# The last four heads' output product by blocks of tokens, its weights in free slots, and the residual's affine step behind the column split

## The chip, the cores and the metric

The kernel runs on one core of a Trainium2 chip. Its time is the device time of one execution in microseconds, the median over runs. A core has TensorE (PE, matrix products, with weight loads as PEld), VectorE (DVE), ScalarE (ACT), GpSimd (POOL) and SyncE (SP, which here issues most DMAs). Each engine works through its own queue in order and waits on semaphores for the others.

## The reference

The program is two small transformer-like blocks of two layers each over 256 latent and 256 context tokens of width 1024. The change touches the end of the first layer (windowed attention with 16 heads) and the beginning of the second (a state-space layer, S5):

```python
o, oc = attention_mixer(p, pc, sink, row, col, True)          # 16 heads of 128
x  = layer_norm(alpha * x  + gate   * ((o  * silu(z))  @ w_out[0]), ln_g[0], ln_b[0])
xc = layer_norm(alpha * xc + gate_c * ((oc * silu(zc)) @ w_out[0]), ln_g[0], ln_b[0])
# layer 1
h  = x  * (1 + scale)   + shift
hc = xc * (1 + scale_c) + shift_c
pz = h @ s5_w_in ; pzc = hc @ s5_w_in                          # then the S5 scan, its gate, w_out[1]
x  = layer_norm(alpha * x + gate * (...), ln_g[1], ln_b[1])
```

## The kernel before

The tokens are four blocks of 128 (0 and 1 latent, 2 and 3 context). All products run in single precision split in two: a value is a high half (rounded, made by ACT, `copy_a`) and a low half (value minus high half, made by a subtraction on DVE or POOL, `sub`), and `mm3` issues three matmuls, high x high, high x low, low x high. A weight unit (`wunit`) is a DMA into one of 6 slots of pool ST, then a high and a low half in one of 3 slots of pool WL. `lo_pat` names, unit by unit, the engine of the low half ("V" for DVE, "P" for POOL).

`l0_attention` runs over the 16 heads: `scores(h + 1)`, `values(h)`, some steps of side generators that prepare the S5 layer, after every fourth head the output product `out_proj(g)` of a finished group of four, and `heads(h + 3)`, the projections of a later head. The product is accumulated in `acc[b]`, one 128x1024 tile for each block. `residual()` multiplies the first three groups' sum by the gate and adds alpha times x. The last group, `out_proj(3)`, comes behind the loop: for each column half `nh`, four blocks `b`; each (nh, b) is 12 matmuls, a product with the gate, a sum into `acc` and `stat` (bn_stats) on DVE. Then `layer_norm` for blocks 0 and 1, and for 2 and 3: thirteen tiny DVE instructions for mean and 1/sigma of two blocks, then one scaling each, on DVE and on ACT. Gain and bias of this norm are not applied here; they are folded into the next layer's columns.

`block1_l1` begins layer 1. `fm_part` transposes the normed blocks (PE), two blocks at a time, latent first, into eight column tiles hT; for each of 8 x 2 parts ACT makes the high half, DVE the scaled value (L384) and, here always DVE, the low half (L385). Beside it POOL does the affine step for the residual, x * ln_g + ln_b, in place on the two latent blocks (L1198 and L1199), and SP stores it to `xrd`, which is read at the end of layer 1. Then `s5_mix` runs its stages in the order of a string: u0 (the first input product, 4 weight units, 96 matmuls), a step of z0, t0, z0, x0, u1, and so on.

Pool E has 8 slots of 128x1024; in layer 0 they hold the eight column tiles of the attention's input, which the projections read. Pool H has 16 such slots. Pools SB and E are closed behind layer 0, and layer 1's pool S5 takes their memory.

The order on each engine is not written out by hand. The program is in the order of the source, and the framework's planner lays out each engine's queue by simulated time (L2030): what is ready and stands earlier in the program goes first. Slots of pools are given out in the same way.

Of the kernel before, what the change touches and what calls it, by code (L numbers as in the profile page):

```python
# [5 lines left out]
F32 = mybir.dt.float32  # L6
F32R = mybir.dt.float32r
# [3 lines left out]
ALU = mybir.AluOpType  # L11
# [94 lines left out]
def bc(ap, *dims):  # L106

    return bass.AP(tensor=ap.tensor, offset=ap.offset, ap=[list(ap.ap[0])] + [list(d) for d in dims])


class Builder:
# [37 lines left out]
        self.nc.scalar.activation(o, i, AF.Copy)  # L149

    def sub(self, o, a, b, eng=None):
        (eng or self.nc.vector).tensor_tensor(o, a, b, op=ALU.subtract)  # L152

    def add(self, o, a, b, eng=None):
        (eng or self.nc.vector).tensor_tensor(o, a, b, op=ALU.add)  # L155

    def mul(self, o, a, b, eng=None):
        (eng or self.nc.vector).tensor_tensor(o, a, b, op=ALU.mult)  # L158

    def ts(self, o, a, s1, op0, s2=None, op1=None, eng=None):  # L160
        e = eng or self.nc.vector
# [198 lines left out]
    def fm_part(self, out, c0, toks, A, B, chunked=False):  # L360


        nc = self.nc
        w = 128 * len(toks)
        m = 512 // w
        for kp in range(8 // m):
            ps = self.pms()
            for k in range(m):
                for b, t in enumerate(toks):
                    kt = m * kp + k  # L370
                    nc.tensor.transpose(ps[:, k * w + b * 128:k * w + (b + 1) * 128], t[:, kt * 128:(kt + 1) * 128],
                                        self.ident)
            h = self.qslot()
            for k in range(m):
                kt = m * kp + k
                sl = slice(k * w, (k + 1) * w)
                src, tmp = ps[:, sl], h[:, sl]
                if chunked:
                    hi, lo = (bc(out[kt][:, r, c0:c0 + 1], (64, 8), (1, 32)) for r in range(2))
                    src, tmp = (bc(t, (1, 8), (8, 32)) for t in (src, tmp))  # L380
                else:
                    hi, lo = (out[kt][:, r, c0:c0 + w] for r in range(2))
                nc.scalar.activation(hi, src, AF.Identity, bias=B(kt), scale=A(kt))
                self.ts(h[:, sl], ps[:, sl], A(kt), ALU.mult, B(kt), ALU.add)  # L384
                self.sub(lo, tmp, hi, nc.gpsimd if k % 2 and not chunked else None)  # L385
            yield

    def layer_norm(self, toks, stats=None, gain=None, bias=None):
# [26 lines left out]
    def l0_attention(self, hT, vps, W, sink, negsink, Wo, gates, ada):  # L415
        nc = self.nc
# [29 lines left out]
        acc, Ks, pend, yz = [], {}, {}, {}  # L446
        sc = 128 ** -0.5

        def heads(h):

            g = h // 4
            if h % 4 == 0:
                Ks[g] = rope(proj(2048 + g * 128))
            q = rope(proj(h * 128))
            zps = proj(3072 + h * 128)
            th = self.qslot()
            nc.scalar.activation(th, zps, AF.Tanh, scale=0.5)
            self.stt(th, th, 1.0, zps, ALU.add, ALU.mult)
            pend[h] = [q, th]
# [46 lines left out]
        def values(h):  # L506
            P, th = pend.pop(h)
            g = h // 4
            PT = []
            for u in range(3):  # L510
                pp = self.pms()
                for k in range(2):
                    for b in range(2):
                        src = P[b][:, (2 * u + k) * 128:(2 * u + k + 1) * 128] if u < 2 else \
                            P[2][:, b * 256 + k * 128:b * 256 + (k + 1) * 128]
                        nc.tensor.transpose(pp[:, k * 256 + b * 128:k * 256 + (b + 1) * 128], src, self.ident)
                if u != 1:
                    pt = self.hslot()
                o = pt[:, 512 * (u % 2):512 * (u % 2 + 1)]
                self.copy_a(o, pp)  # L520
                PT += [o[:, :256], o[:, 256:]]
            yp = self.pms()
            vs = slice(g * 128, (g + 1) * 128)
            for kb in range(4):
                nc.tensor.matmul(yp[:, :256], V[kb][:, vs], PT[kb], start=kb == 0, stop=kb == 3)
            for kb in range(2):
                nc.tensor.matmul(yp[:, 256:], V[2 + kb][:, vs], PT[4 + kb], start=kb == 0, stop=kb == 1)
            self.stt(th, th, 0.5, yp, ALU.mult, ALU.mult)
            y = self.hslot(F32R)[:, :].rearrange("p (a b) -> p a b", a=2)
            self.split(y, th, lo_eng=self.off)  # L530
            yz[h] = y

        def out_proj(g):
            y = [yz.pop(4 * g + k) for k in range(4)]
            if g == 0:
                acc.extend(self.hslot() for _ in range(4))
            gt = gates_
            for nh in range(2):
                ws = [self.w_as(Wo, g * 4 + 2 * u, (nh * 512, 512)) for u in range(2)]
                for b in range(4):  # L540
                    ps = self.pacc()
                    for k in range(4):
                        self.mm3(ps, (y[k][:, 0, b * 128:(b + 1) * 128], y[k][:, 1, b * 128:(b + 1) * 128]),
                                 ws[k // 2][k % 2], k == 0, k == 3)
                    a = acc[b][:, nh * 512:(nh + 1) * 512]
                    if g == 0:
                        self.copy_a(a, ps)
                    elif g < 3:
                        self.add(a, a, ps)
                    else:  # L550
                        t = self.qslot()
                        self.mul(t, ps, gt[b // 2][:, nh * 512:(nh + 1) * 512])
                        self.add(a, a, t)
                        stat(b, nh)

        def residual():

            gates_.extend(gates())
            for b in range(4):
                xt = self.hslot()  # L560
                self.dma(xt, (self.I["x"][0] if b < 2 else self.I["ctx"][0])[(b % 2) * 128:(b % 2 + 1) * 128, :])
                nc.scalar.activation(xt, xt, AF.Copy, scale=ALPHA)
                self.mul(acc[b], acc[b], gates_[b // 2])
                self.add(acc[b], acc[b], xt)

        def stat(b, nh):
            if nh == 0:
                stats[b] = self.T.tile([128, 2, 6], F32, tag="bn", name="bn")
            nc.vector.bn_stats(stats[b][:, nh, :], acc[b][:, nh * 512:(nh + 1) * 512])

        gates_, stats = [], {}
# [7 lines left out]
        for h in range(16):  # L579
            if h < 15:  # L580
                scores(h + 1)
            values(h)
            for k, gen in SIDE[h]:
                for _ in range(k):
                    next(side[gen], None)
            if h % 4 == 1 and h > 3:
                out_proj(h // 4 - 1)
                if h == 13:
                    residual()
            if h + LEAD < 16:  # L590
                heads(h + LEAD)
        self.lo_pat = "P"
        out_proj(3)
        for b in (0, 2):
            self.layer_norm(acc[b:b + 2], [stats[b], stats[b + 1]])
        return acc

    def block1_l0(self):
# [580 lines left out]
    def block1_l1(self):  # L1179
        nc, I = self.nc, self.I  # L1180
        v, at = self.v1, self.v1at
        mod = self.mod1
        A = self.C.tile([128, 2, 2, 8], F32, name="A1")
        for q in range(2):
            g, b = v[:, at["ln_g"]:at["ln_g"] + 8], v[:, at["ln_b"]:at["ln_b"] + 8]
            self.stt(A[:, q, 0, :], mod[:, 8:16, q], 1.0, g, ALU.add, ALU.mult)
            self.stt(A[:, q, 1, :], mod[:, 8:16, q], 1.0, b, ALU.add, ALU.mult)
            self.add(A[:, q, 1, :], A[:, q, 1, :], mod[:, 0:8, q])
        x = self.x1
        hT = [self.hslot(F32R)[:, :].rearrange("p (a b) -> p a b", a=2) for _ in range(8)]  # L1190
        for q in range(2):
            for _ in self.fm_part(hT, 32 * (1 - q), x[2 * q:2 * q + 2], lambda k: A[:, q, 0, k:k + 1], lambda k: A[:, q, 1, k:k + 1], True):
                pass

        xrd = self.DR.tile([256, 1024], F32, name="xrd")
        gb, bb = self.row_bc(I["ln_g"][0]), self.row_bc(I["ln_b"][0])
        for b in range(2):
            self.mul(x[b], x[b], gb, nc.gpsimd)  # L1198
            self.add(x[b], x[b], bb, nc.gpsimd)  # L1199
            self.dma(xrd[b * 128:(b + 1) * 128, :], x[b])  # L1200
        self.xrd = xrd
        return self.s5_mix(hT, I["s5_w_in"][0])
# [831 lines left out]
```

## Time and profile before

| | us |
|---|---|
| median of 3 runs (2323.80 to 2330.18) | 2326.35 |
| the profiled execution | 2329.09 |
| its span | 2327.2 |
| PE busy | 2030.9 |
| DVE busy | 1429.4 |
| ACT busy | 875.5 |
| POOL busy | 749.3 |

The span is what the profiler saw from the first to the last instruction; the execution's own time holds 1.9 us around it. Times within the span count from its start. The seam between the two layers lies between 600 and 745 us.

### The profile page before, as it was taken

What the parts mean: (1) busy time and instruction counts of PE and PEld (TensorE: products, weight loads), DVE (VectorE), ACT (ScalarE), POOL (GpSimd) and SP (SyncE); (2) the same over time, 40 slices, a digit from 0 to 9 for tenths busy, and PEclk for the clock granted to TensorE, in tenths of its full rate; (3) what the DMA queues carried; (4) which work ended last, traced back from release to release, by engine and by line L of the source; (5) the groups of instructions that cost most, each with busy time, mean ns of one, the idle gap of its engine ahead of it and who ended that gap; (6) DMA issues with size and microseconds to landing.
All of it is one profiled execution on the core that took longest, in us unless ns stands there. A gap on an engine that the chain in (4) does not pass through costs nothing. (4 is left out here: it accounts for less than half of the span.)

```text
span 2327.2 us, 34638 instructions
## 1 busy us (share of the span) xinstructions
PE 2030.9 (87%) x13236; PEld 1597.8 (69%) x13236; DVE 1429.4 (61%) x2945; ACT 875.5 (38%) x1650; POOL 749.3 (32%) x501
## 2 busy tenths in 40 slices
PE   5697788999987878659888899999999999988998
PEld 3575565677766676547786565778888877657997
DVE  5788887766695867564547735553333466455556
ACT  2234233334434453534434243343222244334443
POOL 1687877800013201323333210122111513112334
PEclk9897877999998987879999979999999999889999
DMA  7656535544554576989465606433333226354663
GB/s 265 181 181 204 182 110 162 154 164 140 187 165 117 184 182 168 233 193 289 145 231 161 189 15 234 138 91 91 105 95 93 89 75 184 133 175 134 191 190 118
DMA packets 362775, 368.56 MB, mean 158 GB/s; under 512 B 27512, under 2 KB 291420, under 8 KB 362608
## 3 DMA queue, kind: packets, MB, share of 16 engines
q1 hardware_dynamic: 356048, 355.32, 50.9%
q0 software_dynamic: 2208, 6.29, 0.9%
q10 hardware_dynamic: 4352, 4.72, 0.6%
q8 instruction: 105, 1.72, 0.3%
q14 instruction: 62, 0.51, 0.1%
HBM read 319.62 MB, written 46.65 MB: 157 GB/s over the span
## 5 line engine op out<-in xcount | busy, mean ns | idle before, releaser
L149 ACT ACTIVATE wl<-st 128x1024 fp32r<-128x1024 f32 (+1 forms) x332 | 344.4, 1043 | 491.7 <-PE pa L202 165.7
L152 POOL TENSOR_TENSOR wl<-st,wl 128x1024 fp32r<-128x1024 f32 (+1 forms) x98 | 237.3, 2422 | 873.9 <-ACT wl L149 846.8
L152 DVE TENSOR_TENSOR wl<-st,wl 128x1024 fp32r<-128x1024 f32 (+1 forms) x234 | 321.3, 1376 | 269.2 <-ACT wl L149 268.4
L200 PE MATMUL pa<-h,wl 128*128 128x512 f32 (+1 forms) x1152 | 403.5, 353 | 10.5 <-DVE q L158 6.4
L202 PE MATMUL pa<-h,wl 128*128 128x512 f32 (+1 forms) x1152 | 401.6, 350 | 8.0 <-DVE wl L152 7.6
L201 PE MATMUL pa<-h,wl 128*128 128x512 f32 (+1 forms) x1152 | 402.9, 351 | 0.0
L200 PEld LDWEIGHTS pa<-h,wl 128*128 128x128 f32 x1152 | 220.3, 192 | 46.4 <-issue 7.9
L202 PEld LDWEIGHTS pa<-h,wl 128*128 128x128 f32 x1152 | 220.5, 192 | 38.7 <-DVE wl L152 8.7
L201 PEld LDWEIGHTS pa<-h,wl 128*128 128x128 f32 x1152 | 220.8, 192 | 27.8 <-issue 0.2
L201 PE MATMUL pa<-wl,h 128*128 128x512 f32 (+1 forms) x560 | 224.5, 404 | 16.8 <-DVE wl L152 15.3
L200 PE MATMUL pa<-wl,h 128*128 128x512 f32 (+1 forms) x560 | 218.9, 407 | 18.6 <-ACT wl L149 7.4
L202 PE MATMUL pa<-wl,h 128*128 128x512 f32 (+1 forms) x560 | 215.3, 400 | 9.8 <-DVE h L152 5.7
L152 POOL TENSOR_TENSOR h<-q,h 128x256 fp32r<-128x256 f32 (+2 forms) x82 | 95.3, 1170 | 213.4 <-ACT h L149 137.1
L168 DVE SCALAR_TENSOR_TENSOR q<-q,pa 128x512 f32<-128x512 f32 (+1 forms) x104 | 58.9, 567 | 166.7 <-ACT q L1861 91.7
L149 ACT ACTIVATE h<-pm 128x512 f32<-128x512 f32 (+3 forms) x182 | 93.0, 545 | 170.0 <-PE pm L1529 46.4
L201 PE MATMUL pm<-wl,h 128*128 128x512 f32 (+1 forms) x376 | 146.6, 393 | 2.7 <-DVE wl L152 2.0
L200 PEld LDWEIGHTS pa<-wl,h 128*128 128x128 f32 x560 | 110.2, 199 | 55.0 <-ACT h L149 11.4
L202 PE MATMUL pm<-wl,h 128*128 128x512 f32 (+1 forms) x376 | 143.2, 393 | 0.0
L201 PEld LDWEIGHTS pa<-wl,h 128*128 128x128 f32 x560 | 111.7, 199 | 45.3 <-DVE wl L152 18.1
L299 PE MATMUL pf<-st,cs 128*32 128x512 f32 x576 | 98.2, 688 | 50.8 <-DMA st<-in_w_ada_dram 25.0
L200 PE MATMUL pm<-wl,h 128*128 128x512 f32 (+1 forms) x376 | 139.6, 391 | 1.0 <-ACT wl L149 1.0
L202 PEld LDWEIGHTS pa<-wl,h 128*128 128x128 f32 x560 | 109.8, 198 | 35.7 <-DVE h L152 7.2
(352 smaller groups left out, 3768.4 us busy)
## 6 DMA issues: line engine op xcount, KB each, us to landing
st<-in_w_ada_dram SPq DMA_DIRECT2D x96, 512.0 KB, 5.3
st<-in_ada_w_dram SPq DMA_DIRECT2D x48, 512.0 KB, 5.7
st<-in_w_ffn_gate_dram SPq DMA_DIRECT2D x44, 512.0 KB, 4.2
st<-in_w_ffn_up_dram SPq DMA_DIRECT2D x44, 512.0 KB, 3.9
st<-in_w_ffn_down_dram SPq DMA_DIRECT2D x44, 512.0 KB, 3.7
st<-in_attn_w_in_dram SPq DMA_DIRECT2D x40, 512.0 KB, 4.8
st<-in_w_out_dram SPq DMA_DIRECT2D x40, 512.0 KB, 4.0
wd<-w SPq DMA_DIRECT2D x64, 256.0 KB, 4.3
```

The lines of the kernel that those rows point to most:

```text
L149: self.nc.scalar.activation(o, i, AF.Copy)
L152: (eng or self.nc.vector).tensor_tensor(o, a, b, op=ALU.subtract)
L168: self.nc.vector.scalar_tensor_tensor(o, a, s, b, op0=op0, op1=op1)
L200: mm(o, w[0], x[0], start=start, stop=False)
L201: mm(o, w[0], x[1], start=False, stop=False)
L202: mm(o, w[1], x[0], start=False, stop=stop)
L299: mm = nc.tensor.matmul(ps[32 * q:32 * q + 32, :], self.cs[:, blk, kt, :, :], st[:, (q % 2) * 512:(q % 2 + 1) * 512], start=k0 == 0, stop= ...
```

## The change

1. `out_proj` is now only called for the first three groups. Its last-group branch is gone.
2. `last_weights()` loads and splits the last group's four weight units after head 14's values: DMA into ST, high half on ACT, low half on DVE, both into slots of pool E, not of WL.
3. `last_proj()` runs the last product with the blocks outside and the column halves inside, and norms two blocks as soon as both are complete.
4. POOL's first product of the affine step gets an added dependence on the last low half of the columns (`self.last_fm`), and `sub` and `mul` return their instruction for that.

```diff
-                self.sub(lo, tmp, hi, nc.gpsimd if k % 2 and not chunked else None)
+                self.last_fm = self.sub(lo, tmp, hi, nc.gpsimd if k % 2 and not chunked else None)
...
                     if g == 0:
                         self.copy_a(a, ps)
-                    elif g < 3:
+                    else:
                         self.add(a, a, ps)
-                    else:
-                        t = self.qslot()
-                        self.mul(t, ps, gt[b // 2][:, nh * 512:(nh + 1) * 512])
-                        self.add(a, a, t)
-                        stat(b, nh)
+
+        def last_weights():
+
+            ws = []
+            for nh, u in itertools.product(range(2), range(2)):
+                st = self.ST.tile([128, 1024], F32, tag="st", name="st")
+                src = Wo[(12 + 2 * u) * 128:(14 + 2 * u) * 128, nh * 512:nh * 512 + 512].rearrange("(k p) n -> p k n", p=128)
+                self.dma(st[:, :].rearrange("p (a b) -> p a b", b=512), src)
+                hi, lo = (self.hslot(F32R, True) for _ in range(2))
+                self.copy_a(hi, st)
+                self.sub(lo, st, hi)
+                ws.append([(hi[:, k * 512:k * 512 + 512], lo[:, k * 512:k * 512 + 512]) for k in range(2)])
+            return ws
+
+        def last_proj(ws):
+
+            y = [yz.pop(12 + k) for k in range(4)]
+            for b in range(4):
+                for nh in range(2):
+                    ps = self.pacc()
+                    for k in range(4):
+                        self.mm3(ps, (y[k][:, 0, b * 128:(b + 1) * 128], y[k][:, 1, b * 128:(b + 1) * 128]),
+                                 ws[2 * nh + k // 2][k % 2], k == 0, k == 3)
+                    cs = slice(nh * 512, nh * 512 + 512)
+                    t = self.qslot()
+                    self.mul(t, ps, gates_[b // 2][:, cs])
+                    self.add(acc[b][:, cs], acc[b][:, cs], t)
+                    stat(b, nh)
+                if b % 2:
+                    self.layer_norm(acc[b - 1:b + 1], [stats[b - 1], stats[b]])
...
             values(h)
+            if h == 14:
+                lw = last_weights()
...
         self.lo_pat = "P"
-        out_proj(3)
-        for b in (0, 2):
-            self.layer_norm(acc[b:b + 2], [stats[b], stats[b + 1]])
+        last_proj(lw)
         return acc
...
         for b in range(2):
-            self.mul(x[b], x[b], gb, nc.gpsimd)
+            m = self.mul(x[b], x[b], gb, nc.gpsimd)
+            self.tc.add_manual_dep(m.ins, self.last_fm.ins.name,
+                                   mybir.DependencyInfo(mybir.DependencyClass.Sync, mybir.DependencyReason.DATA),
+                                   reason="after the columns")
             self.add(x[b], x[b], bb, nc.gpsimd)
```

## Rows read from the trace of the kernel before

**Rows 1.** Busy time by stretch: stretch, length, busy us (instructions) of PE, PEld, DVE, ACT, POOL, then PEclk, DMA share, GB/s.

```profile
606.00:618.00 12.00, 12.00 (x111) 8.32 (x105) 3.21 (x8) 4.22 (x10) 0.00 (x0) 1.00 0.71 244
...
640.00:680.00 40.00, 32.26 (x232) 24.13 (x231) 36.60 (x58) 16.76 (x31) 4.76 (x2) 0.87 0.50 171
...
679.30:695.20 15.90, 15.89 (x99) 12.45 (x98) 14.54 (x28) 3.87 (x5) 2.54 (x2) 1.00 0.55 146
...
710.00:728.60 18.60, 13.77 (x48) 10.47 (x47) 18.53 (x24) 6.05 (x11) 10.72 (x5) 0.72 0.40 149
728.60:742.00 13.40, 13.40 (x60) 11.07 (x59) 1.23 (x1) 3.96 (x13) 4.56 (x2) 1.00 0.28 89
...
742.00:2327.20 1585.20, 1411.69 (x9585) 1146.17 (x9583) 862.80 (x2045) 615.63 (x1101) 398.31 (x265) 0.92 0.52 152
```

**Rows 2.** Timeline of PE: start, duration, engine, line, operation, count, idle before with its releaser.

```profile
602.94 0.40 PE L202 MATMUL pa<-h,wl 128*128 128x512 f32 x1
...
653.42 0.80 PE L200 MATMUL pa<-wl,h 128*128 128x512 f32 x1 [3.95 <-DVE h L155]
...
702.76 3.68 PE L371 MATMUL pm<-cst,h 128*128 128x128 f32 x16 [7.58 <-DVE h L165]
...
722.41 1.65 PE L202 MATMUL pa<-wl,h 128*128 128x512 f32 x3 [4.05 <-DVE h L152]
...
741.78 0.39 PE L202 MATMUL pm<-wl,h 128*128 128x512 f32 x1
```

**Rows 3.** Timeline of DVE.

```profile
644.18 3.39 DVE L158 TENSOR_TENSOR h<-h 128x1024 f32<-128x1024 f32 x1
...
649.23 3.39 DVE L158 TENSOR_TENSOR h<-h 128x1024 f32<-128x1024 f32 x1
...
678.62 0.68 DVE L152 TENSOR_TENSOR h<-q,h 128x512 fp32r<-128x512 f32 x1
...
713.26 1.13 DVE L152 TENSOR_TENSOR h<-q,h 128x256 fp32r<-128x256 f32 x2
...
720.18 5.28 DVE L152 TENSOR_TENSOR h<-q,h 128x256 fp32r<-128x256 f32 x3
```

**Rows 4.** Costliest groups on DVE, 679.3 to 728.6 us: busy, mean ns, idle before.

```profile
L152 DVE TENSOR_TENSOR h<-q,h 128x256 fp32r<-128x256 f32 x16 | 16.0, 1031 | 0.0
L165 DVE TENSOR_SCALAR q<-pm,A 128x256 f32<-128x256 f32 x16 | 8.1, 541 | 0.4 <-ACT h L383 0.4
L155 DVE TENSOR_TENSOR h<-h,q 128x512 f32<-128x512 f32 x8 | 5.4, 681 | 0.0
L569 DVE BATCH_NORM_STATS2 bn<-h 128x6 f32<-128x512 f32 x8 | 5.4, 679 | 0.0
L158 DVE TENSOR_TENSOR q<-pa,h 128x512 f32<-128x512 f32 x8 | 5.2, 677 | 1.3 <-PE pa L202 1.2
L152 DVE TENSOR_TENSOR wl<-st,wl 128x1024 fp32r<-128x1024 f32 x2 | 2.4, 1213 | 0.0
```

**Rows 5.** Timeline of POOL.

```profile
644.08 2.41 POOL L152 TENSOR_TENSOR wl<-st,wl 128x1024 fp32r<-128x1024 f32 x1 [12.43 <-ACT wl L149]
649.20 2.35 POOL L152 TENSOR_TENSOR wl<-st,wl 128x1024 fp32r<-128x1024 f32 x1 [2.70 <-ACT wl L149]
...
714.42 4.99 POOL L158 TENSOR_TENSOR h<-h 128x1024 f32<-128x1024 f32 x2 [16.90 <-DVE h L152]
719.37 5.17 POOL L155 TENSOR_TENSOR h<-h 128x1024 f32<-128x1024 f32 x2
728.00 2.77 POOL L152 TENSOR_TENSOR wl<-st,wl 128x1024 fp32r<-128x1024 f32 x1 [3.46 <-ACT wl L149]
```

**Rows 6.** Timeline of SP's DMA issues.

```profile
605.90 2.29 SPq L146 DMA_DIRECT2D st<-in_w_out_dram  x4
...
691.91 11.55 SPq L146 DMA_DIRECT2D m<-kd  x16
...
721.99 2.90 SPq L146 DMA_DIRECT2D xrd<-h  x2
...
733.73 7.00 SPq L146 DMA_DIRECT2D st<-wd  x3
```

More of the change, by code (lines that the diff above doesn't have):

```diff
@@ L151, in sub @@
     def sub(self, o, a, b, eng=None):
-        (eng or self.nc.vector).tensor_tensor(o, a, b, op=ALU.subtract)
+        return (eng or self.nc.vector).tensor_tensor(o, a, b, op=ALU.subtract)
     def add(self, o, a, b, eng=None):
@@ L157, in mul @@
     def mul(self, o, a, b, eng=None):
-        (eng or self.nc.vector).tensor_tensor(o, a, b, op=ALU.mult)
+        return (eng or self.nc.vector).tensor_tensor(o, a, b, op=ALU.mult)
     def ts(self, o, a, s1, op0, s2=None, op1=None, eng=None):
@@ L536, in out_proj @@
                 acc.extend(self.hslot() for _ in range(4))
-            gt = gates_
             for nh in range(2):
```

## The prediction

> **What bounds the kernel now.** I read first the table by stretches, because a change at one seam of the kernel can only be priced at that seam. The table splits the span at the points that matter here: the end of head 15, the end of the last product, the end of the column step, the end of the first input product of layer 1 [rows 1]. Up to 742 us the stretch 640 to 680 us shows VectorE (DVE) busy 36.60 of 40 us and TensorE (PE) 32.26; from 679.3 to 695.2 us DVE is busy 14.54 of 15.9 us, and from 710 to 728.6 us 18.53 of 18.6 us while PE has 13.77 and a granted clock of 0.72 [rows 1]. So at this seam DVE sets the pace, and PE waits for it. From 728.6 to 742 us it is the other way round: PE is busy throughout with 60 matmuls in 13.40 us, 0.223 us each, and DVE does one instruction [rows 1].
>
> Then the timeline of PE. After the last product PE stands still for 7.58 us, until the first transposed column at 702.76 us, and inside the first input product of layer 1 (stage u0) for 4.05 us at 722.41 us, both times for DVE; u0 ends at 741.78 + 0.39 = 742.2 us [rows 2]. This is the point that I follow: whatever arrives there earlier or later goes on, since PE has no pause between 728.6 and that end.
>
> Then DVE's work between the end of head 15 (its last subtraction ends at 678.62 + 0.68 = 679.3 us [rows 3]) and the last column subtraction (728.6 us), grouped [rows 4]. Of these 49.3 us, 1.7 are waits, 2.4 are two weight subtractions, and sixteen column subtractions (128x256) take 16.0 us, 1.031 us each [rows 4]. Two of them without a neighbour take 1.13 us together, 0.57 each; three at 720.18 us take 5.28 us, 1.76 each [rows 3]. The slow ones lie beside GpSimd (POOL): its two products and two sums of the affine step run from 714.42 to 724.54 us [rows 5]. The loss there is 16.0 - 16 x 0.57 = 6.9 us.
>
> **The change part by part.**
>
> *Affine step behind the last column.* POOL's four instructions (4.99 + 5.17 = 10.2 us [rows 5]) now wait for DVE's last column subtraction. DVE wins back the 6.9 us. What is queued behind the waiting instruction is the rest of POOL's order: in before the next is the low half of u0's fourth weight unit, 728.00 us, 2.77 us [rows 5], and u0 needs it for its last 24 matmuls. On SP's queue the two stores of the affine result are issued after 721.99 us, and the weights of stage x0 follow at 733.73 us [rows 6]; the stores will be ready some 4 to 6 us later, still ahead of 733.73, so I cost SP at nothing, with 3 us as the upper bound if the x0 loads are put behind a store that comes at 730. x0 starts behind u0, so that cover is several us deep. The affine result itself is read only at the end of layer 1.
>
> *Weights of the last product early, in pool E.* Pool E's eight slots held the eight column tiles, whose last reader is head 15's projection at 602.94 us [rows 2]. The four 512 KB loads that were issued at 605.90 us [rows 6] are issued as before; their four high halves on ScalarE (ACT) and four low halves on DVE can follow at once. Between 606 and 618 us ACT is busy 4.22 and DVE 3.21 of 12 us [rows 1]. A low half costs 1.21 us on DVE [rows 4], so four cost 4.9 us and fit there: I cost them at nothing, and at 4.9 us on DVE if they land between 640 and 680 us instead, where DVE is full. What they remove is POOL's four low halves; two of these, at 644.08 and 649.20 us [rows 5], lie beside the residual's 128x1024 products on DVE, which then take 3.39 us each [rows 3] instead of about 1.2. The WL slots that become free let u0's first three units in early. One of these goes to POOL (about where 644.08 is now) and two to DVE, one of them inside the full stretch: 2.2 us won there, 1.2 spent. PE's stall of 3.95 us at 653.42 us [rows 2], which waits for the residual on DVE and holds up head 15's last scores, shrinks by that. Net: head 15 is done about 1 us earlier (bounds 3 earlier, 4 later).
>
> The two weight subtractions of 2.4 us leave the tail with this, since u0's units are ready before it.
>
> *Blocks outside, column halves inside.* The product keeps its 96 matmuls. Blocks 0 and 1 are finished half way, so their norm and their eight column parts can run while PE multiplies blocks 2 and 3. That takes away the wait of 7.58 us only as far as DVE has room, and it has none: 8 x (product with the gate, sum, statistics) = 5.2 + 5.4 + 5.4 us [rows 4] are already nearly all of the 15.9 us. So I take from this part only DVE's waits (1.7 us), and I pay 0 to 3 us, 1.5 taken, for instructions that stand in DVE's or PE's order ahead of data that aren't there yet. *Norm of a pair at once*: the same instructions as before, two pairs, at no cost. *Pool memory*: layer 1's tiles that reuse E's memory must wait until the weights are free, about 694 us; the sixteen loads at 691.91 us [rows 6] are the first that could feel it, they are read more than 100 us later, so nothing.
>
> *Sum.* DVE from the end of head 15: 49.3 - 1.7 - 2.4 - 6.9 = 38.3 us. Start 679.3 - 1 = 678.3, plus 38.3, plus 1.5: last column at 718.1 us instead of 728.6. Of its last eight parts (each about 0.5 for the scaling and 0.57 for the subtraction, 8.5 us in all) the first two must be there before u0 can run through: 718.1 - 8.5 + 2.1 = 711.7 us. Then u0: 96 x 0.223 = 21.4 us, 12 transposes between (16 took 3.68 us [rows 2], so at most 2.8; I take 2), about 2 us for a restart at the lower of the two clock levels (in before the stretch at 0.72 [rows 1] holds some 10 us at 1.2 GHz in two restarts; now there is one), minus 1 us of high-half products that run ahead. End of u0: 736.1 us. The other path to the same end goes through POOL: 718.1 + 10.2 (affine) + 2.4 (low half) + 24 x 0.223 = 736.1 us, if the planner puts the fourth unit behind the affine step. Both give 742.2 - 736.1 = 6.1 us.
>
> Behind 742 us [rows 1] nothing is edited, and the loads there wait for buffers that PE frees, so I let the 6.1 us pass through whole; a new plan of the later order can move a few us either way. The profiled execution took 2329.09 us, 1.9 more than its span of 2327.2 and 2.7 more than the median of the three runs shown (2326.35); against its time the sum is 2323.0, against the median, which is what is measured, 2320.2. I predict 2320.
>
> **The rivals.**
>
> *A larger gain.* Head 15's chain is sped up by the full 3 us (both residual products undisturbed), no in-order stall, u0's fourth unit ahead of the affine step and no second clock dip: 3 - 1 + 1.5 + 2 + some 2 of PE's transposes moved in front of 695 us, together 7 to 8 us more, 2312. For it: three separate waits are all of the same kind, DVE held up beside POOL. Against it: they must all go right.
>
> *DVE pays for what POOL gives up.* The four low halves fall between 640 and 680 us, where DVE is busy 36.60 of 40 us [rows 1]; head 15 comes 4.9 later instead of 1 earlier. 736.1 + 5.9 = 742: no change, 2326. Decided by where the planner puts them: for it speaks that they stand in the program behind head 14's values, against it the idle ACT and DVE at 606 to 618 us. The Trainium skill, Perfetto Trace Analysis, section Optimizing Scalar/DVE Operations, speaks for this rival: with a saturated DVE, work should be moved off it, to GpSimd if need be, and this change goes the other way. The same section warns that the two share a read port so that moving may not help, and it is this half that the rows of 3.39 us bear out [rows 3].
>
> *POOL's queue becomes the path (slower than before).* u0's end is last column + 10.2 + 2.4 + 5.4 = last column + 18 us. If the columns aren't sped up, this beats PE's own path: at the old 728.6 us it gives 746.6, 4.4 us slower, 2331; with head 15 also 4.9 later, 2336. It decides from a last column at 724 us on. For it: the affine step stands ahead of u0 in the program. Against it: the fourth unit could be ready first and go ahead, and the 6.9 us come back by the very same wait.
>
> *The order does not change as written*: the planner may run blocks 2 and 3 first or keep columns behind all blocks. Since my sum takes next to nothing from the early norm, that gives 2320 to 2322 as well, and needs no chance of its own.
>
> **How the numbers follow.** The forecast (2317 to 2324) has 0.50, the larger gain (2308 to 2316) 0.20, no gain (2324 to 2328) 0.18, slower (2329 to 2337) 0.12. The range leaves out the ends of the outer two: 2309 to 2330. About 0.3%, 7 us, is what a measurement of this kernel can tell from no change: faster than 2319.4 are the larger gain and nearly half of the forecast, 0.43; slower than 2333.3 is some two thirds of the last case, 0.08; the rest, 0.49, is within.
>
> **What would show it right or wrong.** In the profile after: no POOL affine instruction before the last column subtraction, and all sixteen of these near 0.57 us; no PE wait near 4 us inside u0; four weight low halves on DVE soon after 606 us; residual products on DVE near 1.2 us, but for one; last column 10 us, u0's end 6 us earlier, measured from the start. Wrong if the low halves lie after 640 us, if u0's fourth unit waits for POOL, if PE still waits 7 us behind the last product and DVE isn't full there, or if the 6 us are there at u0's end and gone later, in layer 1's recurrences or loads.

## The result and the profile after

Median of the kernel before in the same series 2325.40 us, of the changed kernel 2299.17 us (2285.04 to 2306.04): ratio 0.9883, 95% interval 0.9857 to 0.9909. A second series gave 0.9888 (0.9870 to 0.9907). 26 us were won, where 6 had been forecast, and the result lies below the range. The profiled execution, the slowest of the four, took 2306.04 us with a span of 2304.3.

At the seam the trace shows what the forecast looked for, and a few us more. Busy time by stretch of the changed kernel, against [rows 1]; the third stretch is the beginning of u0, the last two run from 710 us to the last column and from there to the end of u0 (the DMA share, above 1 in some rows, is not used here):

```profile
606.00:618.00 12.00, 12.00 (x115) 8.01 (x108) 7.58 (x9) 8.73 (x15) 0.00 (x0) 1.00 0.89 314
640.00:680.00 40.00, 31.87 (x262) 22.82 (x261) 34.68 (x59) 17.28 (x32) 2.41 (x1) 0.91 0.52 178
...
706.20:710.30 4.10, 3.79 (x12) 2.71 (x10) 4.10 (x10) 2.96 (x7) 0.00 (x0) 0.50 1.27 119
...
710.00:718.10 8.10, 7.80 (x35) 6.49 (x36) 8.02 (x16) 3.21 (x5) 0.67 (x1) 0.95 1.20 165
718.10:731.70 13.60, 13.60 (x63) 11.28 (x62) 1.67 (x1) 4.11 (x14) 13.60 (x6) 1.00 0.41 150
```

The stretch from 606 to 618 us took up the four high halves (ACT 8.73 instead of 4.22 us) and the four low halves (DVE 7.58 instead of 3.21) while PE stays busy for all 12.00 us. Behind 710 us PE has 7.80 of 8.10 us, where it had 13.77 of 18.6; its granted clock of 0.50, the lower of the two levels, is over before that.

Timeline of PE in the changed kernel, against [rows 2]; line 1022 is the first matmul behind u0:

```profile
699.19 1.94 PE L371 MATMUL pm<-cst,h 128*128 128x128 f32 x16 [3.85 <-DVE t L163]
703.53 1.02 PE L371 MATMUL pm<-cst,h 128*128 128x128 f32 x4 [2.40 <-DVE q L165]
705.49 1.09 PE L371 MATMUL pm<-cst,h 128*128 128x128 f32 x4 [0.95 <-DVE q L165]
...
710.30 1.20 PE L202 MATMUL pa<-wl,h 128*128 128x512 f32 x3 [0.31 <-DVE h L152]
...
731.33 0.39 PE L202 MATMUL pm<-wl,h 128*128 128x512 f32 x1
...
734.52 3.95 PE L1022 MATMUL pm<-cst,q 64*64 64x64 f32 x128
```

The pause of 7.58 us is 3.85 now, in front of the transposes (2.40 and 0.95 us follow between them); the one of 4.05 us inside u0 is 0.31. u0 ends at 731.33 + 0.39 = 731.7 us instead of 742.2. The matmul behind u0 begins at 734.52 us; in the kernel before (its line 998) it began here:

```profile
744.98 3.19 PE L998 MATMUL pm<-cst,q 64*64 64x64 f32 x102
```

Timeline of DVE in the changed kernel, against [rows 3]: the four low halves, the first two residual products, the end of head 15, and the last columns:

```profile
611.64 1.23 DVE L152 TENSOR_TENSOR h<-st,h 128x1024 fp32r<-128x1024 f32 x1 [1.36 <-ACT h L149]
613.38 1.22 DVE L152 TENSOR_TENSOR h<-st,h 128x1024 fp32r<-128x1024 f32 x1
615.15 1.23 DVE L152 TENSOR_TENSOR h<-st,h 128x1024 fp32r<-128x1024 f32 x1 [0.55 <-ACT h L149]
616.89 1.22 DVE L152 TENSOR_TENSOR h<-st,h 128x1024 fp32r<-128x1024 f32 x1
...
641.82 2.36 DVE L158 TENSOR_TENSOR h<-h 128x1024 f32<-128x1024 f32 x2 [2.04 <-DMA h<-g]
...
676.99 0.69 DVE L152 TENSOR_TENSOR h<-q,h 128x512 fp32r<-128x512 f32 x1
...
712.54 2.36 DVE L152 TENSOR_TENSOR h<-q,h 128x256 fp32r<-128x256 f32 x4
...
717.42 0.64 DVE L152 TENSOR_TENSOR h<-q,h 128x256 fp32r<-128x256 f32 x1
```

The last column ends at 717.42 + 0.64 = 718.06 us, ten and a half before the 728.6 of [rows 1]. As a group of 677.7 to 718.1 us the sixteen column subtractions read so, against the first line of [rows 4]:

```profile
L152 DVE TENSOR_TENSOR h<-q,h 128x256 fp32r<-128x256 f32 x16 | 9.6, 639 | 0.0
```

639 ns instead of 1031: nothing of POOL lies beside the first fifteen any more, and one of its weight halves starts with the last. Timeline of POOL, against [rows 5]:

```profile
644.66 2.41 POOL L152 TENSOR_TENSOR wl<-st,wl 128x1024 fp32r<-128x1024 f32 x1 [143.68 <-ACT wl L149]
717.43 2.83 POOL L152 TENSOR_TENSOR wl<-st,wl 128x1024 fp32r<-128x1024 f32 x1 [70.37 <-ACT wl L149]
720.22 5.73 POOL L158 TENSOR_TENSOR h<-h 128x1024 f32<-128x1024 f32 x2
725.91 4.75 POOL L155 TENSOR_TENSOR h<-h 128x1024 f32<-128x1024 f32 x2
```

The fourth weight unit of u0 (717.43) stands ahead of the affine step (720.22), not behind it.

So the seam gives 10.5 of the 26 us. Most of the others are in a stage in which no line was edited: the gate stage of layer 1, some 320 us later, where the weights of the gate and of the layer's output product are split into halves. From its first tanh to its last it took 1213.01 - 1060.81 = 152.2 us in the kernel before and 1188.93 - 1049.96 = 139.0 us in the changed one. Busy time by stretch in that stage, before and after (two fences, same columns as above):

```profile
1130.00:1160.00 30.00, 28.02 (x182) 25.34 (x180) 15.20 (x19) 15.32 (x21) 13.10 (x9) 0.94 0.52 155
1160.00:1190.00 30.00, 26.36 (x164) 24.42 (x165) 12.04 (x11) 8.03 (x12) 9.03 (x5) 0.89 0.70 211
```

```profile
1130.00:1160.00 30.00, 30.00 (x212) 28.05 (x210) 15.42 (x20) 14.69 (x22) 15.81 (x11) 1.00 0.71 216
1160.00:1190.00 30.00, 30.00 (x223) 28.73 (x222) 12.16 (x11) 14.51 (x19) 14.23 (x7) 1.00 0.71 224
```

The trace has 435 matmuls of PE in these 60 us instead of 346, at the full granted clock instead of 0.94 and 0.89. What PE waited for most from 1100 to 1200 us (sum, times, longest), before:

```profile
PE pm L202 <- DVE wl L152: 5.6, 3, 2.1
PE pa L201 <- DVE wl L152: 3.6, 3, 2.1
PE pa L200 <- ACT h L149: 2.0, 1, 2.0
```

and after, where no wait for DVE's weight halves is left in this stretch:

```profile
PE pa L200 <- ACT h L149: 2.0, 1, 2.0
PE pm L201 <- POOL wl L152: 0.6, 1, 0.6
```

From the first tanh to the last PE waits 10.6 us for DVE's weight halves before and not at all after; all its waits there add up to 14.9 and 4.4 us. The mean granted clock over the whole stage is 0.96 both times, so the waits are most of the 13 us, and the clock of the 60 us shown is not a gain of the stage as a whole.

**What links the two places.** The helper that loads a weight unit, `wunit`, gives the low half to DVE or POOL by a pattern and a running count: `e = self.lo_pat[self.nlo % len(self.lo_pat)]`, then `self.nlo += 1`. The gate stage sets the pattern to "VVP" and doesn't reset the count. The last product used to take four units through `wunit`; its new function `last_weights` splits by itself and doesn't count. So the gate stage begins at 84 instead of 88, and each round of six units (four of the gate, two of the output product) is shared out V V P V V P instead of V P V V P V. The patterns of two letters in between don't notice a shift by four. The count is reset in the feed-forward part of the second block, so the shift also reaches that block's first mixing layer, which has the same pattern. From the last tanh of the gate stage to the first of the feed-forward part it takes 327.4 to 330.8 us in the seven runs with the old rotation and 327.0 to 328.5 us in the four with the new one: that is not where the gain lies.

### The profile page after: what moved, and what is told of

The parts are those of the page before. It is cut to its first block, busy times and chain, and to the rows that moved or that the text cites. A ratio compares the mean times of both kernels' runs of the same rounds, so it can differ in the third digit from the quotient of the medians.

```text
span 2304.3 us, 34637 instructions
## 1 busy us (share of the span) xinstructions
PE 2014.0 (87%) x13236; PEld 1587.5 (69%) x13236; DVE 1426.6 (62%) x2948; ACT 875.3 (38%) x1650; POOL 744.2 (32%) x498
## 5 line engine op out<-in xcount | busy, mean ns | idle before, releaser
L152 POOL TENSOR_TENSOR wl<-st,wl 128x1024 fp32r<-128x1024 f32 (+1 forms) x95 | 232.3, 2446 | 839.4 <-ACT wl L149 816.5
L152 DVE TENSOR_TENSOR wl<-st,wl 128x1024 fp32r<-128x1024 f32 (+1 forms) x233 | 312.0, 1341 | 242.5 <-ACT wl L149 240.8
L201 PE MATMUL pa<-wl,h 128*128 128x512 f32 (+1 forms) x528 | 211.5, 401 | 11.2 <-DVE wl L152 9.8
L200 PE MATMUL pa<-wl,h 128*128 128x512 f32 (+1 forms) x528 | 206.0, 403 | 8.2 <-ACT h L149 4.1
L202 PE MATMUL pa<-wl,h 128*128 128x512 f32 (+1 forms) x528 | 203.2, 396 | 6.5 <-POOL h L152 5.6
L201 PEld LDWEIGHTS pa<-wl,h 128*128 128x128 f32 x528 | 105.1, 199 | 38.0 <-DVE wl L152 11.5
L200 PEld LDWEIGHTS pa<-wl,h 128*128 128x128 f32 x528 | 104.1, 198 | 38.9 <-ACT h L149 8.5
L202 PEld LDWEIGHTS pa<-wl,h 128*128 128x128 f32 x528 | 103.6, 197 | 30.0 <-POOL h L152 6.4
```

The lines of the kernel that those rows point to most:

```text
L152: return (eng or self.nc.vector).tensor_tensor(o, a, b, op=ALU.subtract)
L200: mm(o, w[0], x[0], start=start, stop=False)
L201: mm(o, w[0], x[1], start=False, stop=False)
L202: mm(o, w[1], x[0], start=False, stop=stop)
```

## The experiments

Two stretches of the trace serve as gauges, since they are free of what came earlier in an execution (the last product of head 13's values begins anywhere from 609 to 617 us). *Seam*: from the last product of head 15's values (line 527 before) to the first matmul behind u0 (line 998 before). *Gate*: from the first to the last of the sixteen tanh of the gate stage. Both are differences of two starts in the timelines of PE and ACT. "Before" is the median of the kernel before in the same series.

| run | median us | before | ratio, 95% | seam us | gate us |
|---|---|---|---|---|---|
| before, first profile | | | | 70.4 | 152.2 |
| e5 before again | one run, 2320.36 | | | 70.6 | 149.5 |
| changed kernel | 2299.17 | 2325.40 | 0.9883 (0.9857-0.9909) | 61.0 | 139.0 |
| e6 changed again | 2297.67 | 2324.77 | 0.9888 (0.9870-0.9907) | 61.3 | 137.8 |
| e1 rotation only | 2305.04 | 2320.96 | 0.9937 (0.9921-0.9954) | 67.0 | 135.4 |
| e2 rotation undone | 2308.68 | 2320.96 | 0.9951 (0.9933-0.9969) | 60.8 | 151.6 |
| e3 third rotation | 2299.53 | 2320.96 | 0.9903 (0.9887-0.9919) | 60.5 | 141.7 |
| e4 wait only | 2315.20 | 2320.96 | 0.9975 (0.9956-0.9993) | 63.7 | 149.4 |
| e7 no wait | 2313.17 | 2324.77 | 0.9959 (0.9944-0.9975) | 63.8 | 154.4 |
| e8 old order | 2314.17 | 2324.77 | 0.9956 (0.9938-0.9973) | 61.4 | 154.3 |
| e9 early weights only | 2319.82 | 2324.88 | 0.9976 (0.9958-0.9993) | 66.7 | 153.1 |
| e10 VectorE from the gate stage on | 2286.23 | 2324.88 | 0.9853 (0.9826-0.9879) | 60.6 | 131.9 |
| e11 wait and rotation | 2296.03 | 2324.88 | 0.9874 (0.9851-0.9898) | 64.1 | 134.2 |
| e12 VectorE up to the feed-forward | 2292.19 | 2328.70 | 0.9846 (0.9825-0.9867) | 61.5 | 134.3 |
| e13 wait and VectorE | 2297.16 | 2328.70 | 0.9871 (0.9850-0.9892) | 63.8 | 131.2 |

**e1, e2, e3: the count alone, undone, and its third position.** Theory A: the rotation causes the gain behind 742 us. Rival B: the earlier seam does, by shifting what collides there.

```diff
     def block1_glu(self, G):
...
         self.lo_pat = "VVP"
+        self.nlo += 2    # e1, in the kernel before: the changed kernel's rotation
+        self.nlo += 4    # e2, in the changed kernel: the rotation of before
+        self.nlo += 2    # e3, in the changed kernel: P V V P V V
```

> The kernel before, with one count shifted: the weight units of the gate stage at the end of layer 1 take their engines from the pattern V, V, P by a running count. The change removes four counted units ahead of it, which turns the pattern by one place there (from V P V V P V to V V P V V P over each six units); here the count alone is shifted, the seam between the layers stays as before. Theory A (two gains: about 11 us at the seam, and the rest, 12 to 15 us, from the turned pattern in the gate stage): 2325 - 13 = 2312 us. Theory B (the gain behind the seam is an echo of the earlier arrival in loads and plan): no change, 2325 us.

> The changed kernel, with the count set back by four units ahead of the gate stage, so that this stage has the engines of before. Theory A: the seam's gain alone, 2325 - 11 = 2314 us, and the gate stage ends about 11 us earlier than before, not 24. Theory B: as the changed kernel, about 2299 us.

> The changed kernel with the pattern of the gate stage in its third position (P V V P V V over each six units). Theory A: a third value that the pattern sets, between 2290 and 2320 us, other than 2299 by some us. Theory B: as the changed kernel, about 2299 us.

One added line, without any of the change, gives 0.9937, 15 us by the ratio and 16 by the medians, where theory A asked for 13; the change without its shifted count keeps 11 to 12 of its 26 us. Theory A holds from both sides in e1 and e2. e3 comes out as its theory B had it, 2299.53 us: in time the third position can't be told from the changed kernel's, so e3 alone decides nothing, and what is slow is the old position. The gate gauge says the same: 149.4 to 154.4 us in all seven runs with the old rotation, 134.2 to 139.0 in the four with the new, 141.7 with the third, whatever the seam is.

**e4: the wait of the affine step alone.**

```diff
-            self.mul(x[b], x[b], gb, nc.gpsimd)
+            m = self.mul(x[b], x[b], gb, nc.gpsimd)
+            self.tc.add_manual_dep(m.ins, self.last_fm.ins.name, ...)
```

> The kernel before with the affine step's wait alone: GpSimd's four instructions behind the last column subtraction, nothing else. Theory A (VectorE sets the pace of the columns, and GpSimd beside it costs 6.9 us): the sixteen column subtractions near 0.57 us each, the end of the first input product of layer 1 4 to 6 us earlier, 2320 us. Rival (the columns aren't the path, or GpSimd's fourth weight unit behind the affine step takes the gain): 2324 to 2328 us.

0.9975, 6 us, where the forecast's term stood at 6.9 less what POOL's queue would take back; the seam is 6.7 us shorter. The queue took nothing back, since the fourth unit's low half ran ahead of the affine step (POOL began it at 721.59 us, the step at 724.37).

**e5: the kernel before a second time**, as a gauge of the gauges.

> The kernel before, unchanged, for a second profile of it. Theory A (what the changed kernel wins at the seam, 10.5 us at the first matmul behind u0, comes from its edits): the second profile has that matmul (line 998) within 2 us of the first profile's 745.0, and head 15's last value within 1 us. Rival B (executions of the same code differ by several us at the seam): line 998 comes 4 to 6 us earlier or later than in the first profile, as it did in the run with the rotation alone (5.3 earlier), whose code is the same up to there; then the seam's gain must be taken from medians alone.

Line 998 is at 744.98 us again, though head 13's values began 1.7 us earlier: theory A. The 67.0 of e1, whose lines are the same up to the gate stage, lies outside what these two show (70.4 and 70.6), but two profiles don't bound the scatter. What its trace shows there is a weight half of the next stage that DVE makes at 727.96 us and here at 732.48; whether its changed count reaches back that far, through the plan of the order, stays open.

**e6, e7, e8, e9: the parts of the seam**, the last three with the old rotation of the gate stage.

```diff
# e7: the changed kernel without add_manual_dep
# e8: the changed kernel, product in the old order
-            for b in range(4):
-                for nh in range(2):
+            for nh in range(2):
+                for b in range(4):
...
-                if b % 2:
-                    self.layer_norm(acc[b - 1:b + 1], [stats[b - 1], stats[b]])
+            for b in (0, 2):
+                self.layer_norm(acc[b:b + 2], [stats[b], stats[b + 1]])
# e9: both
```

> The changed kernel, unchanged, beside the kernel before on the same chip as the next two. Sum of the parts measured so far: rotation alone 16 us, everything else 12 us, together 28, so a ratio near 0.988 (2293 against 2321). Rival: with the rotation undone in the changed kernel 12 us were left of 26, so the rotation would be worth 14 and the sum 26: 0.9888; both lie in one interval. Above 0.992 the parts would not add up.

> The new order of the last product and its early weights, without the wait of the affine step; the rotation of the later weight halves as in the kernel before. With the wait it took 12 us off, and the wait alone 6. Theory A (the two add): 6 us less than before, 2315. Rival B (without the wait the columns still run beside the affine step at 1.8 us each, and they end the seam whatever the product does): no gain, 2319 to 2323, with the three columns beside POOL again at 5 us together. Rival C (the early weights and the early norm do nearly all): 10 to 12 us less, 2309.

> The early weights and the wait, but the product with the halves of its columns outside and the norms at its end, as before; the rotation of the later weight halves as in the kernel before. The full change with that rotation took 12 us off, the wait alone 6. Theory A (as in the prediction, the order of the blocks gives next to nothing, the early weights free DVE from POOL): 11 to 12 us less, 2309, and PE's pause behind the product's last matmul is 7 us again while its end comes earlier. Rival B (the pause of 7.6 us, which shrank to 3.9, is the rest of the gain): 6 to 8 us less, 2314, so the early weights give 0 to 2.

> Of the whole change only the early weights of the last product: no wait of the affine step, the old order of the product, the norms at its end, and the rotation of the later weight halves as before. The wait without the early weights took 6 us off, the early weights with the wait or with the new order 11. Theory A (the early weights hold the memory that the affine step's two vectors are loaded into, so the step starts behind the columns with or without the wait): 9 to 12 us less, about 2314, POOL's first affine instruction at 714 us or later, last column near 718. Rival B (it needs the wait or the new order): affine step at 710 to 713 us, three columns of 1.8 us beside it, 0 to 5 us less, about 2321.

e6: the parts add up. e8: the order of the blocks and the early norm give nothing that shows (61.4 against 60.8 us at the seam, 0.9956 against 0.9951): in time theory A, as in the prediction. Its sign, a pause of 7 us again, was wrong: PE's pause behind the product is 4.44 us in e8 and in e9, so it is mainly the early weights that shorten the 7.58, not the early norm. e7: 9.5 us less by the ratio and 11.6 by the medians, nearest to theory C, and not to be told from e2 with the wait (0.9951). In its trace 3 us of seam are lost without the wait, yet only one column, the last, is slowed by the affine step and takes 2.52 us. Why only one, e9 shows with its POOL:

```profile
720.30 5.02 POOL L158 TENSOR_TENSOR h<-h 128x1024 f32<-128x1024 f32 x2 [70.57 <-DMA h<-in_ln_g_dram]
725.29 5.72 POOL L155 TENSOR_TENSOR h<-h 128x1024 f32<-128x1024 f32 x2
730.98 4.67 POOL L152 TENSOR_TENSOR wl<-st,wl 128x1024 fp32r<-128x1024 f32 x2
```

The affine step waits for its own vector. On SP's queue the loads of the two vectors stand behind the sixteen `m<-kd`, which reuse pool E's memory, now full of weights: SP's queue waited 11.3 us for PE's last product, which ended at 695.3 us, and issued the first load into that memory at 695.40. SP's issues in the changed kernel, against [rows 6]:

```profile
606.78 2.27 SPq L146 DMA_DIRECT2D st<-in_w_out_dram  x4
...
696.09 12.97 SPq L146 DMA_DIRECT2D m<-kd  x16
709.82 0.35 SPq L146 DMA_DIRECT2D h<-in_ln_g_dram  x1
...
728.33 2.68 SPq L146 DMA_DIRECT2D xrd<-h  x2
```

The sixteen are 4.2 us later than in [rows 6], and with them the vector (it was issued at 705.90 us in the kernel before). So the early weights hold the affine step back by themselves, and the written wait and this one overlap. In e7 and e9 there is no wait that lets the fourth unit go first, and the rival of the prediction that had POOL's queue as the path appears: PE waits 2.69 us for that unit in e7, about the 3 us by which its seam is longer, and 2.84 us in e9, in PE's timeline:

```profile
733.36 0.50 PE L201 MATMUL pa<-wl,h 128*128 128x512 f32 x1 [2.84 <-POOL wl L152]
```

e9's median is 5 us below before, half of what theory A asked for and at the edge of rival B's range. Theory A's mechanism is there (affine step from 720.30 us on, only the last column slowed), but not its last column near 718 us: it ends at 723.1, and this wait costs another 2.84 us.

**e10, e12: why the rotation matters.** Is it the place of each half in the round, or POOL beside DVE?

```diff
     def block1_glu(self, G):
...
-        self.lo_pat = "VVP"
+        self.lo_pat = "V"      # e10; e12 sets "VVP" again where the feed-forward resets nlo
```

> The changed kernel with all low halves of the gate stage's weights on VectorE, none on GpSimd. Theory A (the rotation's gain is that VectorE's halves, 1.72 us each beside GpSimd in the kernel before and 1.32 in the changed one, come late for TensorE): halves at 1.22 us, no wait of TensorE for them above 1 us, and the time of the changed kernel or up to 5 us less, 2293 to 2298. Rival B (what counts is which engine has which place in the six units; VectorE with all six is late again): TensorE waits 5 us and more for them, 4 to 12 us more than the changed kernel, 2302 to 2310.

> The changed kernel with VectorE alone for the low halves of the gate stage and of what lies between it and the feed-forward loops, which keep the pattern of before. (In the run with VectorE alone for the gate stage the pattern stayed in force in the feed-forward loops too; that run was 11 us below the changed kernel.) Theory A (the gain is that of the gate stage, GpSimd's halves there slow VectorE's): 2286 to 2290, ratio 0.985 to 0.987. Rival B (the gain comes from the feed-forward loops): that of the changed kernel, 2296 to 2299, ratio 0.9885.

0.9853 and 0.9846: theory A in both, 8 to 10 us below the changed kernel (0.9853 / 0.9888 = 0.9965 and 0.9846 / 0.9888 = 0.9958), the fastest of all. The interval of e12 lies clear of the changed kernel's, that of e10 overlaps it a little. e10 is faster than its theory A said (2293 to 2298); in the gate stage its PE waits once for a half of DVE, 0.8 us. In e10 the pattern stays in force in the feed-forward loops, which its expectation did not say; e12 leaves these as they were, so the gain isn't theirs. The gate gauge shows 3.5 to 7 of the 8 to 10 us; where the others lie is not shown. DVE takes all halves and has time for them. The weight halves from 1100 to 1180 us as groups (count, busy, mean ns, idle before), kernel before:

```profile
L152 DVE TENSOR_TENSOR wl<-st,wl 128x1024 fp32r<-128x1024 f32 x14 | 23.9, 1716 | 20.0 <-ACT wl L149 20.0
...
L152 POOL TENSOR_TENSOR wl<-st,wl 128x1024 fp32r<-128x1024 f32 x8 | 19.5, 2434 | 44.4 <-ACT wl L149 44.4
```

the changed kernel:

```profile
L152 DVE TENSOR_TENSOR wl<-st,wl 128x1024 fp32r<-128x1024 f32 x18 | 23.6, 1311 | 23.3 <-ACT wl L149 23.2
L152 POOL TENSOR_TENSOR wl<-st,wl 128x1024 fp32r<-128x1024 f32 x9 | 22.1, 2453 | 22.6 <-ACT wl L149 22.5
```

and e12:

```profile
L152 DVE TENSOR_TENSOR wl<-st,wl 128x1024 fp32r<-128x1024 f32 x29 | 35.1, 1226 | 20.4 <-ACT wl L149 20.2
```

The mean falls from 1716 to 1311 ns although POOL has no fewer halves (9 and 8), so it is their place that counts, and to 1226 ns where POOL has none. How one of POOL's halves holds DVE up is seen in the timelines of POOL, DVE and PE of the kernel before:

```profile
1157.12 2.38 POOL L152 TENSOR_TENSOR wl<-st,wl 128x1024 fp32r<-128x1024 f32 x1 [3.20 <-ACT wl L149]
...
1158.02 3.69 DVE L152 TENSOR_TENSOR wl<-st,wl 128x1024 fp32r<-128x1024 f32 x2 [4.92 <-ACT wl L149]
...
1160.64 0.51 PE L202 MATMUL pm<-h,wl 128*128 128x256 f32 x1 [2.09 <-DVE wl L152]
```

ACT makes the high halves in close succession. POOL gets the first and starts at 1157.12; DVE gets the next at 1158.02 and needs 3.69 us for two halves that take 1.23 each elsewhere: 1157.12 + 2.38 = 1159.50, and two more halves end at 1161.71. It stood still until POOL was done, and PE waited 2.09 us for it. In the changed kernel DVE gets the first of such a run, and POOL comes behind:

```profile
1144.57 1.23 DVE L152 TENSOR_TENSOR wl<-st,wl 128x1024 fp32r<-128x1024 f32 x1 [2.93 <-ACT wl L149]
...
1145.56 2.50 POOL L152 TENSOR_TENSOR wl<-st,wl 128x1024 fp32r<-128x1024 f32 x1 [3.11 <-ACT wl L149]
```

This is no single case. Between the first tanh and the last, 11 of DVE's weight halves start while a half of POOL runs in each of the seven runs with the old rotation, most of them 0.9 us behind it. In the four with the new one 5 or 6 do, most of them 1.8 us behind it, in e3 one, in e10, e12 and e13 none. Whether DVE began 0.9 or 2 us behind POOL, its half ended 1.08 to 1.09 us after POOL's, each time. So the old position of the pattern puts more halves of DVE behind a half of POOL, and closer behind its start. Why the third position, with one such half, still takes 141.7 us is not shown; PE waits 4.7 us for ACT's high halves there.

The Trainium skill, SBUF — State Buffer, section SBUF: two separate sides, says that the two engines share a pair of ports as an exclusive lock: of a VectorE instruction with two inputs in SBUF and a GpSimd instruction, whichever starts first holds it for its whole instruction. The trace agrees: the end 1.08 us after POOL's, whenever DVE began.

**e11, e13: the wait without the new product.** Line for line the kernel before, with e4's wait and e1's count, or with e4's wait and e10's pattern.

> The kernel before with the wait of the affine step and the changed kernel's rotation, and nothing of the last product's change. Theory A (the parts add): 6 + 16 = 22 us less, about 2302, ratio 0.9905. Rival B (the new product is needed for the rest): against the changed kernel's ratio of 0.9885 this one gives 0.992 or more.

> The kernel before with the wait of the affine step and VectorE alone for the low halves from the gate stage on, and nothing of the last product's change. Theory A (with the wait there, the new product gives nothing more that can be measured): the ratio of the changed product with VectorE alone, 0.985, so 2289 against 2324. Rival B (the product adds the 3 to 4 us by which the first matmul behind u0 lies earlier in its traces): 0.9868, 2293. Rival C (it adds 6 us, as the medians without the rotation say): 0.988 or more.

e11 is at 0.9874, no slower than the whole change (0.9888): theory A, and even below its sum. e13 is at 0.9871 against 0.9853 and 0.9846 with the new product: nearest to rival B. With the wait in both kernels, the new product shortens the seam by 2 to 3 us in every pair of traces (63.7 to 60.8, 64.1 to 61.3, 63.8 to 61.5); in the totals that gives 6, -3 and 4 to 6 us, so its size is open within a few us, while the wait and the count carry the rest.

## Why the prediction was wrong

**The step that failed** is "Behind 742 us nothing is edited ... so I let the 6.1 us pass through whole; a new plan of the later order can move a few us either way". No line was edited there, but a value was: the running count that shares out the low halves. The gate stage became 13 us shorter (152.2 to 139.0), and e1 and e2 put 16 and 26 - 12 = 14 us on the count. This isn't the planner's chance, which the sentence allowed for: it is there in every run with that rotation, and could have been counted from the code, four calls of `wunit` less in front of a pattern of three. The rows to price it were in the trace of before as well: DVE's halves of 1716 ns beside POOL, and PE's waits for them.

**The seam, term by term.** Head 15's end: 1 us earlier forecast, 676.99 + 0.69 = 677.7 against 679.3, 1.6. Four low halves hidden at 606 to 618 us: so. Residual products undisturbed: 2.36 us for two instead of 3.39 each. The affine step's 6.9 us on DVE: 16.0 - 9.6 = 6.4. (The row of three subtractions in 5.28 us is not 1.76 each: two took 4.75 together, and the third, behind POOL's end, 0.60.) DVE from there to the last column: 38.3 + 1.5 forecast, 718.06 - 677.7 = 40.4 measured. Last column at 718.1 forecast, 718.06 measured; that it is so near is in part luck, since head 15 came 0.6 us earlier than forecast and DVE took 0.6 us longer. DVE has no room for the early norm: so, e8 shows nothing lost without it.

**Mis-sized: from the last column to the end of u0.** Forecast 18 us, both by PE and by POOL, measured 731.7 - 718.06 = 13.6 (the stretch above, PE busy throughout), so u0 ended 10.5 us earlier instead of 6.1. On PE's side the terms were taken one after the other (711.7 + 21.4 + 2 + 2 - 1), whereas u0 began at 706.2 us at the lower clock level and was at the higher one from 710.8 us on, before the last columns came. On POOL's side the planner put the fourth unit in front of the affine step; the rival "larger gain" had named that. The rival that made POOL's queue the path is real only without the written wait (e7, e9).

**Costed at nothing for the wrong reason.** The sixteen `m<-kd` loads were expected late and without effect, since they are read 100 us later. They were 4.2 us late, and what they held back was the load queued behind them, the affine step's vector. Without the written wait (e7, e9) that kept the step from slowing any column but the last; with it, no effect shows.

**The rival with DVE paying** fell: the halves landed where DVE was idle. The Trainium skill, Perfetto Trace Analysis, section Optimizing Scalar/DVE Operations, had been set beside it. What the section says is that with a saturated DVE moving some work off it, even to GpSimd, may make sense, but might not help, since the two share a read port. Where e10 and e12 move weight halves the other way they win, which fits the second half. The first is not tested by them: in the gate stage of before DVE was busy 69.67 of 152.2 us.

**What is left of the 26.** u0's end gives 10.5 (of it 1 from head 15 and 9.4 in the seam's gauge), the gate stage 13.2 in the first pair of traces and 11.7 in e5 and e6. The other 2 to 4 lie in stretches whose own length varies by more than that from run to run: from the first matmul behind u0 to the first tanh it is 308.6 (e2) to 316.8 us (e5), so no cause is named for them.

**The chances**: "within 0.3%" was held the likeliest, and faster at 0.43. The seam's part alone (e2, 0.9951, 11 to 12 us) is what the rival "larger gain" had, at 0.20, and twice the 6 us of the forecast.

## What to carry to other kernels

When an edit removes calls of a helper, look for the state that the helper keeps (a running count, a slot, a pattern): it reaches stages that the diff doesn't show, and its effect may be larger than that of the edit. Where weight halves that become ready in close succession go to VectorE and GpSimd, VectorE's should start first, or all should be VectorE's while it has room. And a wait in the right place can be worth more than a new order: the new order of the product showed no gain of its own (e8), the wait alone 6 us (e4), and one dependency and one count gave 0.9874 where the whole change, which has both, gave 0.9888.

## What the runs showed of the hardware

A subtraction of two tensors on VectorE doesn't get slower in proportion beside GpSimd, it stands still until GpSimd's instruction ends: a weight half of 1.23 us took 1.43 to 2.59 us in the gate stage of the kernel before, and each of the 11 ended 1.08 to 1.09 us after GpSimd's half, however early it had begun. An instruction of one tensor, from PSUM, and two scalars per row is not held up: in the kernel before, DVE's timeline beside the affine step (POOL from 714.42 to 724.54 us) reads

```profile
715.22 2.02 DVE L152 TENSOR_TENSOR h<-q,h 128x256 fp32r<-128x256 f32 x1
717.16 0.52 DVE L165 TENSOR_SCALAR q<-pm,A 128x256 f32<-128x256 f32 x1
717.61 2.20 DVE L152 TENSOR_TENSOR h<-q,h 128x256 fp32r<-128x256 f32 x1
719.73 0.53 DVE L165 TENSOR_SCALAR q<-pm,A 128x256 f32<-128x256 f32 x1
720.18 4.75 DVE L152 TENSOR_TENSOR h<-q,h 128x256 fp32r<-128x256 f32 x2
```

Taking work from GpSimd and giving all of it to VectorE, 29 halves instead of 14 in 80 us, made each shorter (1226 against 1716 ns). From 1130 to 1190 us PE's granted clock was 1.00 in the changed kernel, where it had been 0.94 and 0.89 with the waits in between; over the whole gate stage it was 0.96 in both.
